# Other columns for the operands of the last nine passes of a decoder step, one pass with a gap in its columns and one with its products in another order

## The chip, the cores and the metric

The kernel runs on one core of a Trainium2 chip. The metric is the time of one execution on the device in microseconds, measured over several runs of the whole program; three runs of the kernel before gave 1616.21, 1616.83 and 1617.44 us, with a median of 1616.83 us.

## The reference

One layer of a decoder for a group of 256 prompt tokens and a group of 32 sample tokens, 288 rows in all, with a model width of 2048. What bears on the change is its end:

```python
merged = gates[:, :, 0] * y_conv + gates[:, :, 1] * y_sb + gates[:, :, 2] * y_mem
x = x + merged @ p['w_o']
h2 = rms_norm(x, p['g_mlp'])
x = x + jnp.square(jax.nn.relu(h2 @ p['w_up'])) @ p['w_down']
```

`w_o` is 2048 by 2048, `w_up` 2048 by 8192 and `w_down` 8192 by 2048. Before these lines stand the combined projection, a convolution branch, stick-breaking attention and attention into a memory, none of which the change touches.

## The kernel before

All activations are held transposed: 128 features on the partitions, the 288 tokens along the columns (T = 288). A product of 128 output features is one "tile": 16 blocks of 128 input features, each with a 128x128 block of weights as the stationary operand and the 128x288 activations as the moving operand, accumulated in one bank of PSUM.

The weights are kept in float32 in HBM and TensorE is used in its fp32r type, so every operand is split in a high part (rounded to fp32r) and a low part (the rest). Each block of a tile is three matmuls: high weights by high activations, high weights by low activations, low weights by high activations. A slab is 8 blocks of weights side by side (128 x 1024 columns, 512 KB); there are 504 of them, and each is loaded by a DMA from SP's queue into a buffer `wr` (line 285), rounded on ScalarE into `wh` (line 307), and subtracted on VectorE into `wl` (line 318). `wr`, `wh` and `wl` have four buffers each. The generator `products` (line 544) issues a slab's 24 matmuls through `chunk` (line 536, the matmul is line 538): first the 16 with `wh`, going through the blocks with the high and the low activations in turn, then the 8 with `wl`. A tile of the last passes is two slabs, 48 matmuls.

The last nine passes are the output projection (`out_tile`, line 1388, 16 tiles) and, for each of four quarters c = 0 to 3 of the 8192 hidden features, an up pass (`up_tile`, line 1423, 16 tiles) and a down pass (`down_tile`, line 1441, 16 tiles). An up tile is evacuated by VectorE (line 1427, relu and scale), squared on GpSimd (line 1430), rounded to the high part on ScalarE (line 1433), and its low part is taken on VectorE (line 1435). These two parts are the moving operands of the down pass that follows. They lie in 16 pairs of "homes" that `make_homes` (line 1327) cuts out of two older buffer pools, `k4` (ten tiles of 1024 columns, three homes in each, 320 columns apart) and `s` (eight tiles of 512 columns, one home in each). The output projection's moving operands lie in the same homes, written by `branch` (line 1354). The moving operands of the up passes are the normalised activations `h2`, in tiles `a` of 320 columns.

Where in these buffers an operand starts is set by constants (line 176 and line 179): `AHEAD = 4` is the first column in a tile `a`, `HOME = 36` the first column of a home, and `SHIFT = 5` the first column of a slab's parts in `wh` and `wl` (line 288, tiles of 1088 columns), except for the 16 slabs of the memory stage, which start at column 0. In the memory stage (line 591) the roles are turned: the weights are the moving operand, 512 columns wide, and the activations, from column 32 of their tiles, are stationary.

The order of all instructions is worked out before the program is built: generators ask a planner (`Order`) for time on an engine, with costs such as `MM = 0.131` us per matmul, and the planner puts each engine's instructions in a fixed order. A matmul group is planned no earlier than the flags of the operands it uses: both parts of its slab and its activations.

Of the kernel before, what the change touches and what calls it, by code (L numbers as in the profile page):

```python
# [8 lines left out]
F32R = mybir.dt.float32r  # L9
# [6 lines left out]
P = 128  # L16
D_MODEL = 2048
KT = D_MODEL // P
# [4 lines left out]
T = NP + NS  # L23
# [14 lines left out]
N_SLABS = 504  # L38
# [134 lines left out]


APART = 320
AHEAD, HOME = 4, 36
PAD = 64
GRP = 32
SHIFT = 5
MM = 0.131  # L180
MM_MEM = 0.226

# [2 lines left out]
def tile_decoder_step(ctx: ExitStack, tc: tile.TileContext, xT, memT, wall, cvec, kmat, ptab,  # L185
                      kpool, vpool, mkc, mvc, hist,
                      yT, oK, oV, oCp, oCs, oMK, oMV):
    nc = tc.nc
# [20 lines left out]
    def tl(p, shape, dt=F32):  # L209
        cnt[0] += 1  # L210
        return pools[p].tile(shape, dt, tag=p, name=f"{p}_{cnt[0]}")
# [27 lines left out]
    first = cm[:, C_BGATE:C_BGATE + 2 * ML].rearrange("p (k t) -> p k t", k=2)  # L239
# [31 lines left out]
    class Slab:  # L271
        def __init__(self, parts):
            self.parts = parts
            self.landed = [Flag() for _ in range(parts)]
            self.split = [Flag() for _ in range(parts)]
# [11 lines left out]

    def shifted(p, s):
        n = 0 if s < 2 * KT // 2 else SHIFT
        return tl(p, [P, SLAB + PAD], F32R)[:, n:n + SLAB]  # L290

    def due(s):
# [242 lines left out]

    def chunk(ps, todo, first, last):
        for i, (w, a) in enumerate(todo):
            nc.tensor.matmul(ps, w, a, start=(first and i == 0), stop=(last and i == len(todo) - 1))  # L538

    slab_no = [0]  # L540
    FULL = [k * P for k in range(8)]
# [2 lines left out]
    def products(ps, uses, acts, first=True, last=True, n=T):  # L544

        s = slab_no[0] - 1
        sl = slabs[s]
        high = [(sl.h, c, a, x) for c, a in zip(uses, acts) for x in (0, 1)]
        low = [(sl.l, c, a, 0) for c, a in zip(uses, acts)]
        todo = high + low  # L550
        for i in range(0, len(todo), STEP):
            part = todo[i:i + STEP]
            yield pe(len(part) * MM, *sl.split, *{a.flag for _, _, a, _ in part})
            if i == 0 and first:
                start_slab(s)
            chunk(ps, [(w[:, c:c + P], a.l if x else a.h) for w, c, a, x in part],
                  first and i == 0, last and i + STEP >= len(todo))

    def main_tile(acts, evac, rank=1.0, n_slabs=2):
        yield pe(0.0, pm=1)  # L560
        ps = bank("pm")[:, :T]
        for i in range(n_slabs):
            slab_no[0] += 1
            yield from products(ps, FULL, acts[8 * i:8 * i + 8], i == 0, i == n_slabs - 1)
            give("w")
        add(evac(ps), rank)
# [754 lines left out]
    homes, homes_in = [], Flag()  # L1321

    class Home:
        def __init__(self, h, l):
            self.h, self.l = h, l

    def make_homes():
        yield sp(*conv_done, *osb_in, k4=bufs["k4"], s=bufs["s"])
        parts = []
        for _ in range(bufs["k4"]):  # L1330
            x = tl("k4", [P, 1024], F32R)
            parts += [x[:, HOME + i * APART:HOME + i * APART + T] for i in range(3)]
        for _ in range(bufs["s"]):
            parts.append(tl("s", [P, 512], F32R)[:, HOME:HOME + T])
        for j in range(KT):
            homes.append(Home(parts[2 * j], parts[2 * j + 1]))
        done(homes_in)


# [12 lines left out]
    merged = [None] * KT  # L1352

    def branch(br, j):
        def evac(ps):
            sig = gates[br, j]
            if br == 2:
                yield dve(T, sig.flag, a=1)
                macc[j] = tl("a", [P, T])
                nc.vector.tensor_mul(macc[j], ps, sig.out)  # L1360
                give("pm")
                give("t")
                return
            yield dve(T, sig.flag)
            nc.vector.tensor_mul(sig.out, ps, sig.out)
            give("pm")
            yield dve(T)
            nc.vector.tensor_add(macc[j], macc[j], sig.out)
            give("t")
            if br == 0:  # L1370
                yield act(T, homes_in)
                a = merged[j] = homes[j]
                nc.scalar.copy(a.h, macc[j])
                yield dve(T)
                nc.vector.tensor_sub(a.l, macc[j], a.h.bitcast(F32))
                give("a")
                done(merged_in[j])
        return evac
# [41 lines left out]
        return load, evac  # L1420


    def up_tile(u, f):
        def evac(ps):
            yield dve(T, r2_done, t=1)
            r = tl("t", [P, T])
            nc.vector.scalar_tensor_tensor(r, ps, 0.0, r2, op0=ALU.max, op1=ALU.mult)  # L1427
            give("pm")
            yield pool(T)
            nc.gpsimd.tensor_mul(r, r, r)  # L1430
            yield act(T)
            a = homes[f]
            nc.scalar.copy(a.h, r)  # L1433
            yield dve(T)
            nc.vector.tensor_sub(a.l, r, a.h.bitcast(F32))  # L1435
            give("t")
            u[f].h, u[f].l = a.h, a.l
            done(u[f].flag)
        return evac
# [57 lines left out]
    def main():  # L1497
        yield from warm_up()
        yield from mem_products()
        yield from conv_products([evac_lin(0, "pa"), evac_gat(0, "pa"), evac_lin(1, "pm"), evac_gat(1, "pm")])  # L1500
        for j in range(2, CT):
            yield from main_tile(hx, evac_lin(j, "pm"))
            yield from main_tile(hx, evac_gat(j, "pm"))
        add(samples(), 2.3)
        for h in range(MH):
            yield from main_tile(hx, mem_head(h), 2 + 0.05 * h)
        for h in range(SH):
            yield from main_tile(hx, sb_key(h), 2.2 + 0.05 * h)
            yield from main_tile(hx, sb_query(h), 2.2 + 0.05 * h)
            yield from main_tile(hx, sb_head(h), 2.2 + 0.05 * h)  # L1510
        yield from branch_products(2, [Late(omem, h, om_in[h]) for h in range(MH)])
        give("a", 8)
        yield from branch_products(1, [Late(osb, h, osb_in[h]) for h in range(SH)])
        give("a", 16)
        yield from branch_products(0, [Late(cact, j, cact_flags[j]) for j in range(CT)])
        give("a", 40)
        mg = [Late(merged, j, merged_in[j]) for j in range(KT)]
        for j in range(KT):
            load, evac = out_tile(j)
            add(load(), 2)  # L1520
            yield from main_tile(mg, evac)
        add(after(sums_2, x1_norm), 0.4)
        hh = [Late(h2, j, h2_in[j]) for j in range(KT)]
        for c in range(D_FF // D_MODEL):
            u = [Later() for _ in range(KT)]
            for f in range(KT):
                yield from main_tile(hh, up_tile(u, f))
            for j in range(KT):
                yield from main_tile(u, down_tile(j, c == D_FF // D_MODEL - 1))

# [167 lines left out]
```

## Time and profile before

| what | value |
|---|---|
| median of three runs | 1616.83 us |
| the profiled execution | 1617.72 us |
| its span, first to last instruction | 1615.9 us |
| PE busy | 1610.4 us, 12638 matmuls |
| VectorE busy | 978.3 us |
| ScalarE busy | 752.6 us |
| GpSimd busy | 139.6 us |
| mean of the DMA traffic | 192 GB/s |

The profile is of one execution. Its span leaves out some 1.8 us of the execution's own time, before the first and after the last instruction. Rows of the views name an engine, a line of the kernel, the operation and its operands as output <- inputs by the names of their pools. For `pm<-k,wh` the output is a bank of the pool `pm`, the moving operand lies in a tile of `k4` and the stationary operand in `wh`. "PEld" is the loading of a stationary operand, which is recorded beside the matmul. The recorded length of a matmul is from its start to its last result, and matmuls overlap; how many follow each other in how much time is read from their starts. A timeline row gives the start, the length, the engine and how many alike instructions were merged in it.

### The profile page before, as it was taken

To read this page: it belongs to the slowest core of one execution; us is meant where nothing else is said; L and a number is where in the kernel's file an instruction comes from. 1 tells how busy PE (TensorE), PEld (TensorE's weight loads), DVE (VectorE), ACT (ScalarE), POOL (GpSimd) and SP (SyncE) were. 2 spreads that over 40 slices of the span, in tenths; PEclk is the share of its full clock that TensorE was granted. 3 is DMA by queue.
4 is the path that set the end of the run, shared out by engine and by line. 5 is a ranking of instruction groups with operands and counts; after the bars stand their busy time and mean duration, and the time that the engine had idled before them with its cause. 6 is when DMAs were issued, how large, how long until landed. Compare 5 with 4: busy or idle time off the path is not lost.

```text
span 1615.9 us, 30749 instructions
## 1 busy us (share of the span) xinstructions
PE 1610.4 (100%) x12638; PEld 1592.4 (99%) x12638; DVE 978.3 (61%) x1503; ACT 752.6 (47%) x1078; POOL 139.6 (9%) x106
## 2 busy tenths in 40 slices
PE   9999999999999999999999999999999999999999
PEld 7999999999999999999999999999999999999999
DVE  7889888877777655655555544555445554455443
ACT  8856877654334534444443333333333333333332
POOL 0020000000000000002222100121002210022100
PEclk9999999999999999999999999999999999999999
DMA  9887778987755555466655555555555555555562
GB/s 326 231 198 267 201 256 237 323 225 271 220 170 166 173 169 170 151 195 191 193 171 167 170 170 169 168 170 171 169 170 170 170 170 169 171 167 169 180 194 95
DMA packets 127200, 310.25 MB, mean 192 GB/s; under 512 B 40018, under 2 KB 49618, under 8 KB 127058
## 3 DMA queue, kind: packets, MB, share of 16 engines
q1 hardware_dynamic: 126770, 307.98, 61.2%
q8 instruction: 99, 1.62, 0.4%
q10 hardware_dynamic: 288, 0.29, 0.1%
q14 instruction: 43, 0.35, 0.1%
HBM read 296.99 MB, written 6.32 MB: 188 GB/s over the span
## 4 chain that ended last, share of the span: by engine, by line
PE 97%; DVE 1%; DMA 1%; issue 0%; ACT 0%; SPq 0%; DVEq 0%; ACTq 0%
PE pm L538 91%; PE pm L591 3%; DMA wr<-in_wall 1%; PE pa L538 1%; PE pl L1090 1%; DVE wl L318 1%; PE pl L1274 0%; PE pa L917 0%; PE pa L919 0%; PE pa L918 0%; PE pl L1104 0%; DVE a L770 0%; PE pa L1214 0%; PE pa L1250 0%; ACT wh L307 0%
## 5 line engine op out<-in xcount | busy, mean ns | idle before, releaser
L307 ACT CAST wh<-wr 128x1024 fp32r<-128x1024 f32 (+1 forms) x520 | 529.2, 1022 | 643.3 <-PE pm L538 570.6
L318 DVE TENSOR_TENSOR wl<-wr,wh 128x1024 fp32r<-128x1024 f32 (+1 forms) x520 | 618.2, 1193 | 192.6 <-ACT wh L307 189.6
L538 PE MATMUL pm<-a,wh 128*128 128x288 f32 x5184 | 733.9, 292 | 0.0
L538 PEld LDWEIGHTS pm<-a,wh 128*128 128x128 f32 x5184 | 695.2, 188 | 1.4 <-issue 1.0
L538 PE MATMUL pm<-a,wl 128*128 128x288 f32 x2592 | 394.9, 292 | 0.0
L538 PEld LDWEIGHTS pm<-a,wl 128*128 128x128 f32 x2592 | 358.0, 188 | 0.0
L538 PE MATMUL pm<-k,wh 128*128 128x288 f32 x2400 | 338.0, 292 | 0.0
L538 PEld LDWEIGHTS pm<-k,wh 128*128 128x128 f32 x2400 | 321.6, 188 | 0.0
L538 PE MATMUL pm<-k,wl 128*128 128x288 f32 x1200 | 181.8, 292 | 0.0
L538 PEld LDWEIGHTS pm<-k,wl 128*128 128x128 f32 x1200 | 165.4, 188 | 0.0
L1430 POOL TENSOR_TENSOR t<-t 128x288 f32<-128x288 f32 x64 | 96.7, 1510 | 599.2 <-DVE t L1427 599.2
L1444 DVE TENSOR_TENSOR a<-a,pm 128x288 f32<-128x288 f32 x64 | 29.0, 454 | 122.7 <-PE pm L538 122.7
L1427 DVE SCALAR_TENSOR_TENSOR t<-pm,rx 128x288 f32<-128x288 f32 x64 | 29.3, 457 | 92.1 <-PE pm L538 92.1
L1433 ACT CAST k<-t 128x288 fp32r<-128x288 f32 x60 | 26.0, 433 | 126.0 <-POOL t L1430 126.0
L1346 DVE TENSOR_TENSOR t<-pm,rx 128x288 f32<-128x288 f32 x48 | 22.0, 458 | 71.8 <-PE pm L538 71.8
L1435 DVE TENSOR_TENSOR k<-t,k 128x288 fp32r<-128x288 f32 x60 | 28.0, 466 | 59.4 <-ACT k L1433 59.4
L770 DVE SCALAR_TENSOR_TENSOR a<-a,cv,a 128x256 f32<-128x256 f32 x120 | 59.5, 496 | 1.4
L1416 POOL TENSOR_TENSOR t<-t,t 128x288 f32<-128x288 f32 x15 | 21.9, 1462 | 413.9 <-ACT t L1413 413.9
L591 PE MATMUL pm<-wh,a 128*128 128x512 f32 x128 | 34.8, 392 | 0.5 <-ACT wh L307 0.5
L538 PE MATMUL pm<-s,wh 128*128 128x288 f32 x160 | 33.8, 292 | 0.0
L591 PEld LDWEIGHTS pm<-wh,a 128*128 128x128 f32 x128 | 24.1, 190 | 6.5 <-ACT wh L307 1.6
L538 PEld LDWEIGHTS pm<-s,wh 128*128 128x128 f32 x160 | 25.6, 188 | 0.0
(181 smaller groups left out, 707.7 us busy)
## 6 DMA issues: line engine op xcount, KB each, us to landing
wr<-in_wall SPq DMA_DIRECT2D x488, 512.0 KB, 3.7
wr<-in_wall SPq DMA_DIRECT2D x32, 256.0 KB, 5.1
k<-in_kpool SPq DMA_DIRECT2D x32, 256.0 KB, 5.9
k<-in_vpool SPq DMA_DIRECT2D x32, 256.0 KB, 5.9
k<-in_mkc SPq DMA_DIRECT2D x8, 512.0 KB, 8.9
k<-in_mvc SPq DMA_DIRECT2D x8, 512.0 KB, 8.2
t<-in_xT SPq DMA_DIRECT2D x16, 144.0 KB, 3.7
out_yT<-a SPq DMA_DIRECT2D x16, 144.0 KB, 1.9
```

The lines of the kernel that those rows point to most:

```text
L307: nc.scalar.copy(sl.h[:, c], sl.raw[:, c])
L318: nc.vector.tensor_sub(sl.l[:, c], sl.raw[:, c], sl.h[:, c].bitcast(F32))
L538: nc.tensor.matmul(ps, w, a, start=(first and i == 0), stop=(last and i == len(todo) - 1))
L591: nc.tensor.matmul(ps[m], y[:, m * P:(m + 1) * P], z[:, w], start=(k == 0 and j < 2), stop=(k == KT - 1 and j in (4, 5)))
L770: nc.vector.scalar_tensor_tensor(c[:, :NP], up[:, k:k + NP], w, c[:, :NP], op0=ALU.mult, op1=ALU.add)
L1346: nc.vector.tensor_mul(g, ps, rx)
L1416: nc.gpsimd.tensor_add(sq_sum[0], sq_sum[0], res[0])
L1427: nc.vector.scalar_tensor_tensor(r, ps, 0.0, r2, op0=ALU.max, op1=ALU.mult)
L1430: nc.gpsimd.tensor_mul(r, r, r)
L1433: nc.scalar.copy(a.h, r)
L1435: nc.vector.tensor_sub(a.l, r, a.h.bitcast(F32))
L1444: nc.vector.tensor_add(x1[j], x1[j], ps)
```

## The change

Six things are changed, all in the last nine passes.

- A home is now 320 columns, starting at column 32 of its slot, and each pass says where in it the operand starts. The output projection's operands start 12 columns in. The four down passes start at 0, 4, 8 and 16 columns in.
- The weights of these passes are shifted along: 13 columns for the output projection, and one more than the activations for the down passes, so 1, 5, 9 and 17.
- The weights of the first up pass start at column 37 in place of 5; the other three up passes keep 5.
- In the second down pass (c = 1) the 288 moving columns have a gap: 144 columns, 16 unused ones, 144 columns. ScalarE and VectorE write them so, and the matmul reads them and writes PSUM with a two-part pattern (PSUM itself has no gap).
- In the last quarter (c = 3, up and down) the 24 products of a slab come in another order: for each block high weights by high activations, low weights by high activations, high weights by low activations, where before all 16 with the high weights came ahead of the 8 with the low ones.
- `HOME` goes from 36 to 32, which is part of the first point.

```diff
-AHEAD, HOME = 4, 36
+AHEAD, HOME = 4, 32
...
+FF0 = N_SLABS - 4 * 4 * KT
+OUT_AT = 12
+DOWN_AT = (0, 4, 8, 16)
+DOWN_GAP = (0, 16, 0, 0)
+UP_SHIFT = (37, 5, 5, 5)
...
     def shifted(p, s):
         n = 0 if s < 2 * KT // 2 else SHIFT
+        if FF0 - 2 * KT <= s < FF0:
+            n = OUT_AT + 1
+        elif s >= FF0:
+            c, i = divmod(s - FF0, 4 * KT)
+            n = UP_SHIFT[c] if i < 2 * KT else DOWN_AT[c] + 1
         return tl(p, [P, SLAB + PAD], F32R)[:, n:n + SLAB]
...
-            nc.tensor.matmul(ps, w, a, start=(first and i == 0), stop=(last and i == len(todo) - 1))
+            nc.tensor.matmul(like(ps, a), w, a, start=(first and i == 0), stop=(last and i == len(todo) - 1))
...
         todo = high + low
+        if s >= FF0 + 3 * 4 * KT:
+            todo = [x for i, y in enumerate(low) for x in (high[2 * i], y, high[2 * i + 1])]
...
     class Home:
-        def __init__(self, h, l):
-            self.h, self.l = h, l
+        def __init__(self, j, at, gap=0):
+            self.h, self.l = (apart(x[:, at:at + T], gap) for x in homes[j])
+
+    def apart(x, gap):
+        if not gap:
+            return x
+        return bass.AP(tensor=x.tensor, offset=x.offset, ap=[list(x.ap[0]), [T // 2 + gap, 2], [1, T // 2]])
+
+    def like(x, a):
+        return x if len(a.shape) == 2 else x.rearrange("p (i t) -> p i t", i=2)
...
-                a = merged[j] = homes[j]
+                a = merged[j] = Home(j, OUT_AT)
...
-            a = homes[f]
+            a = Home(f, DOWN_AT[c], DOWN_GAP[c])
+            r = like(r, a.h)
```

More of the change, by code (lines that the diff above doesn't have):

```diff
@@ L1331, in make_homes @@
             x = tl("k4", [P, 1024], F32R)
-            parts += [x[:, HOME + i * APART:HOME + i * APART + T] for i in range(3)]
+            parts += [x[:, HOME + i * APART:HOME + (i + 1) * APART] for i in range(3)]
         for _ in range(bufs["s"]):
-            parts.append(tl("s", [P, 512], F32R)[:, HOME:HOME + T])
+            parts.append(tl("s", [P, 512], F32R)[:, HOME:HOME + APART])
         for j in range(KT):
-            homes.append(Home(parts[2 * j], parts[2 * j + 1]))
+            homes.append(parts[2 * j:2 * j + 2])
         done(homes_in)
@@ L1420, in out_tile, with up_tile @@
         return load, evac
-    def up_tile(u, f):
+    def up_tile(u, f, c):
         def evac(ps):
@@ L1526, in main @@
             for f in range(KT):
-                yield from main_tile(hh, up_tile(u, f))
+                yield from main_tile(hh, up_tile(u, f, c))
             for j in range(KT):
```

## Prediction, made before the changed kernel was run

> **What bounds the kernel now.** I read the page first (who is busy, which chain ended last), then the chain of waits in order of time and PE's waits, then the busy time by passes.
>
> ```profile
> span 1615.9 us, 30749 instructions
> PE 1610.4 (100%) x12638; PEld 1592.4 (99%) x12638; DVE 978.3 (61%) x1503; ACT 752.6 (47%) x1078; POOL 139.6 (9%) x106
> PE 97%; DVE 1%; DMA 1%; issue 0%; ACT 0%; SPq 0%; DVEq 0%; ACTq 0%
> L538 PEld LDWEIGHTS pm<-a,wh 128*128 128x128 f32 x5184 | 695.2, 188 | 1.4 <-issue 1.0
> ```
>
> PE is busy for the whole span and carries 97% of the chain. A busy PE says little by itself, since overlapping matmuls count as busy; whether it waits is seen in the next two views, the chain and PE's waits.
>
> ```profile
> 422.81 3.70 PE pl L1090 x128
> 426.52 1185.81 PE pm L538 x9120
> 1612.35 0.46 DVE a L1444
> PE pa L1494 <- PEq L1675: 0.8, 1, 0.8
> PE pa L919 <- DVE a L898: 0.7, 1, 0.7
> PE pm L591 <- ACT wh L307: 0.5, 2, 0.3
> ```
>
> From 426.52 us to the end the chain is one piece: 9120 matmuls of line 538 in 1185.81 us, which is 130.02 ns each, and then one evacuation. PE waits three times in the whole program, all earlier. So the only thing that can move this kernel's end, as long as no new wait appears, is how fast one matmul follows another. The windows view, cut at the nine changed passes (output projection, then up and down four times), shows that rate for each pass:
>
> ```profile
> 713.59:813.43 99.84, 99.84 (x770) 99.84 (x769) 1.00 0.61 193
> 813.43:913.27 99.84, 99.84 (x770) 99.84 (x769) 1.00 0.54 168
> 913.27:1013.12 99.85, 99.85 (x771) 99.85 (x770) 1.00 0.54 170
> 1013.12:1112.95 99.83, 99.83 (x770) 99.83 (x769) 1.00 0.54 168
> ...
> 1512.31:1612.15 99.84, 99.84 (x770) 99.78 (x768) 1.00 0.50 159
> ```
>
> The columns are the stretch, its length, PE's and PEld's busy time, the granted clock, the DMA share and GB/s. Each pass takes 99.84 us for its 16 x 48 = 768 matmuls (the x770 counts the ones that overlap an edge): 130.0 ns each, at the full clock, whatever else is going on. The nine passes are 6912 matmuls and 898.6 us, so **one ns per matmul in all of them is 6.9 us (0.43%), in one pass 0.77 us**. About 0.2%, 3.2 us, is what a measurement of this kernel can tell from no change.
>
> **Part by part: places of the columns.** Nothing is added or removed: the same 6912 matmuls read the same number of columns. What can change is the 130.0 ns, if it depends on where the moving columns and the columns being loaded as stationary operand lie. By the code all tiles concerned are multiples of 64 columns wide (1024, 512, 320 apart, 1088, 320), so every buffer of a pool has the same place modulo 64. The kernel before holds three arrangements, as stationary start less moving start: 5 - 4 = 1 in the up passes, 5 - 36 = -31 in the output projection and the down passes, and 32 - 0 in the memory stage. The windows show the first two equal to 0.01 us in a pass, and that over every k, s and a buffer. For the third there is the timeline of the memory stage:
>
> ```profile
> 19.98 1.07 PE L591 MATMUL pm<-wh,a 128*128 128x512 f32 x4
> ...
> 44.45 1.07 PE L591 MATMUL pm<-wh,a 128*128 128x512 f32 x4
> ```
>
> Between these two rows lie 18 groups of 6 matmuls (4 with the weights' high part, 2 with the low): 24.47 us / 108 = 226.6 ns for 512 columns, 0.4425 ns a column, against 130.0 / 288 = 0.4514. A straight line through both is 5.8 ns fixed and 0.4313 ns a column. So no arrangement in this trace is visibly dearer.
>
> After the change the difference is 13 - 44 = -31 for the output projection, 1 - 32, 5 - 36, 9 - 40 and 17 - 48 = -31 for the down passes, all as before: both operands are moved together, by +8, -4, 0, +4 and +12 columns. The first up pass goes from 1 to 37 - 4 = 33, which modulo 64 is the -31 that the down passes run at already. If it is the difference that counts, these edits cost nothing. That the common place doesn't count is not shown by any row, since the trace has only starts 4, 36 and 0 for the moving columns. Bounds: if the new places freed all of the fixed part that the memory row suggests, a matmul would take 288 x 0.4425 = 127.4 ns, 2.6 ns less, 2.0 us a pass. If they brought a collision that kept a load from lying beside the matmul ahead of it, the 188 ns of the LDWEIGHTS row would be the least, 58 ns more, 44.5 us a pass; that is far from anything seen, since 188 is a recorded length with its start and end, and PEld is 99% busy at 130 ns all the same. I take 0, since the three arrangements seen are nearest.
>
> **The gap.** In the second down pass the moving operand is 2 x 144 columns. The nearest rows are two products with samples, both 64 matmuls with 32 stationary and 256 moving columns; line 1104 reads the 256 in one piece, line 1274 in two pieces of 128 that lie apart:
>
> ```profile
> 148.36 3.66 PE L1104 MATMUL pl<-k,k 128*32 128x256 f32 x64
> 296.92 3.64 PE L1274 MATMUL pl<-k,k 128*32 128x256 f32 x64
> ```
>
> 3.64 us against 3.66: two pieces cost nothing, down to 0.3 ns a matmul. Paid once more at the worst, the fixed 5.8 ns would be 4.5 us for the pass. I take 0.
>
> **The order in the last quarter.** Its loads alternate between wh and wl where before the same wh block was loaded twice in a row. Within a slab before, both kinds already stand: 16 matmuls in which the stationary block repeats and 8 in which it never does.
>
> ```profile
> 1509.19 2.24 PE L538 MATMUL pm<-a,wh 128*128 128x288 f32 x16
> 1511.27 1.20 PE L538 MATMUL pm<-a,wl 128*128 128x288 f32 x8
> 1512.31 2.24 PE L538 MATMUL pm<-k,wh 128*128 128x288 f32 x16
> ```
>
> From start to start 2.08 us / 16 and 1.04 us / 8: 130.0 ns both. So the order costs nothing in rate; bounds as above, by 2.6 ns x 1536 = 4.0 us either way. It also shifts two waits. wl of a slab is needed by its 2nd matmul, not its 17th, 15 x 0.13 = 2.0 us earlier. And the last use of wh is the 24th matmul, not the 16th, so that ScalarE's rounding of the slab four later, which waits for that buffer, starts up to 8 x 0.13 = 1.04 us later. Queued behind it in order are the rounding of an up tile (line 1433) and the next slab's; VectorE's subtraction, and with it the wr buffer for SP's next DMA, follow it. The timeline about the last pass's start gives the cover:
>
> ```profile
> 1461.55 1.05 ACT L307 CAST wh<-wr 128x1024 fp32r<-128x1024 f32 x1 [1.67 <-PE pm L538]
> 1462.97 1.22 DVE L318 TENSOR_TENSOR wl<-wr,wh 128x1024 fp32r<-128x1024 f32 x1
> 1471.75 2.24 PE L538 MATMUL pm<-a,wh 128*128 128x288 f32 x16
> 1514.66 0.43 ACT L1433 CAST s<-t 128x288 fp32r<-128x288 f32 x1 [2.14 <-POOL t L1430]
> 1515.13 0.46 DVE L1435 TENSOR_TENSOR s<-t,s 128x288 fp32r<-128x288 f32 x1 [1.02 <-ACT s L1433]
> 1517.25 0.42 PE L538 MATMUL pm<-s,wh 128*128 128x288 f32 x2
> ```
>
> The slab rounded at 1461.55 has its low part at 1464.19 and is used from 1471.75: 7.6 us, of which at most 1.04 go with the later start, and the 2.0 us of wl's earlier need have no bearing, as the slab's first matmul already stands 7 us behind. The ACT rows show 1.67 and 2.14 us idle ahead of these instructions, which take up the shift, so the up tile's rounding stays where GpSimd lets it go. The last up tile's parts are ready at 1515.59 and read from 1517.25; in the new order their block is the 45th and not the 39th in the pass's first tile, 0.8 us later, so the slack grows. For the loads:
>
> ```profile
> wr<-in_wall SPq DMA_DIRECT2D x488, 512.0 KB, 3.7
> ```
>
> A wr buffer set free at 1464.19 + 1.04 is filled again 3.7 us after its issue, about 1469, for a rounding at 1461.55 + 4 x 3.12 = 1474.0. Were all this cover gone, it would cost up to 1.04 us at each of the 64 slabs; with 5 us left I take 0.
>
> **The sum** is 0 + 0 + 0 against the profiled execution's 1617.72 us (span 1615.9 and 1.8 around it), which is 0.9 above the median of the runs. Carried to the median: **1616.8 us**.
>
> **The rivals.** (a) *The common place counts, for the worse.* In the passes where both operands are moved or split (output projection and four down passes, 3840 matmuls) the moving stream and the load behind it meet. Price: the only difference per matmul that placements show here, 2.6 ns, the other way, is 10.0 us, 1626.8; with the gap at 5.8 in place of 2.6 ns it is 12.4 us, 1629.2. It decides from 3.2 us / 3840 = 0.84 ns a matmul. For it: starts 0, 8, 12 and 16 stand in no row. Against it: starts 4 and 36, and k, s and a buffers, agree to 0.01 us in a pass. (b) *The common place or the order frees some of the fixed part.* The same 3840 matmuls at -2.6 ns give -10.0 us, 1606.8; the last quarter's order alone -4.0 us, 1612.8. For it: 512 columns take less per column. Against it: that is explained as well by a fixed part that no place removes. The Trainium skill ("TensorE: Matmul & The Clock Gate", Back-to-back issue gap) puts a warm gap at N / 2.4 + 2.5 ns, an estimate of 122.5 ns for 288 columns; by that, 7.5 of the 130.0 ns could go, 29 us in these passes, 1588. The trace disagrees with it in every arrangement (226.6 ns for 512 columns against 215.8), so I give such a gain hardly anything. (c) *The change doesn't do what it says*, as the difference modulo 64 stays -31 nearly everywhere: this has the same time as my forecast and is counted in it.
>
> **How the numbers follow.** No change 0.50, since every row at hand gives 130.0; (a) 0.27, as the new common places are untested and the starting one is at least not bad; (b) 0.23. That gives faster 0.23, same 0.50, slower 0.27. The forecast's own range is 1613.6 to 1620.0. The whole range goes from (b)'s 1606.8 to (a)'s 1629.2: it leaves out a collision much dearer than 2.6 ns (about 0.10) and a gain as large as the far part of (b) (about 0.08).
>
> **What would show it.** Right: windows cut at the passes again give 99.84 us each, in all nine, and PE waits nowhere after 426 us. Wrong by (a) or (b): single passes differ, those moved in common from the two up passes that are left alone (c = 1 and 2), and the windows name the pass: 97.8 us for -2.6 ns, 101.8 for +2.6. If the first up pass alone differs, modulo 64 was the mistake; if the last up pass differs, which has only the new order, the order was; if only the gap's pass does, the two-piece read. A wait of PE on wl or wh in the last quarter would prove the cover wrong.

## The result, and the profile after

The changed kernel takes 1630.68 us in the median of four runs (1630.51 to 1631.61), the kernel before, with a fourth run added, 1616.66 us: a ratio of 1.0087, with a 95% interval of 1.0075 to 1.0099. It is 14.0 us slower. The forecast was no change, and the time lies 1.5 us above the range.

The page's head, then the end of the chain and all of PE's waits:

```profile
span 1629.8 us, 30749 instructions
PE 1624.0 (100%) x12638; PEld 1606.4 (99%) x12638; DVE 982.3 (60%) x1503; ACT 754.2 (46%) x1078; POOL 126.0 (8%) x106
```

```profile
426.65 1199.65 PE pm L548 x9120
```

```profile
PE pa L931 <- DVE a L910: 1.5, 1, 1.5
PE pa L1515 <- PEq L1696: 0.8, 1, 0.8
```

The number of instructions is the same, the last piece of the chain is again 9120 matmuls in one run, and PE waits for nothing after 426 us: of its two waits one is the first matmul's, at 0.8 us, and the other ends at 128.35 us. But the piece is 13.84 us longer, 131.5 ns a matmul in place of 130.0. Where, the windows show, cut at the starts of the nine passes (output projection, then up and down for c = 0 to 3; stretch, length, PE and PEld busy, clock, DMA share, GB/s):

```profile
713.73:813.58 99.85, 99.85 (x771) 99.85 (x769) 1.00 0.61 193
813.58:915.98 102.40, 102.40 (x771) 102.40 (x770) 1.00 0.53 165
915.98:1018.38 102.40, 102.40 (x771) 102.40 (x770) 1.00 0.53 165
1018.38:1118.21 99.83, 99.83 (x770) 99.83 (x769) 1.00 0.55 169
1118.21:1221.64 103.43, 103.43 (x771) 103.43 (x770) 1.00 0.53 164
1221.64:1321.48 99.84, 99.84 (x770) 99.84 (x769) 1.00 0.54 168
1321.48:1423.88 102.40, 102.40 (x770) 102.40 (x769) 1.00 0.52 166
1423.88:1523.73 99.85, 99.85 (x771) 99.85 (x769) 1.00 0.55 168
1523.73:1626.12 102.39, 102.39 (x770) 102.32 (x768) 1.00 0.49 156
```

Four passes are as before, 130.0 ns a matmul: the output projection at columns 12 and 13, the two up passes that were left alone, and the last up pass, which has only the new order. Four others take 102.40 us, 133.33 ns: the first up pass with its weights at 37, and the down passes at 0, 8 and 16. The pass with the gap takes 103.43 us, 134.67 ns. 4 x 2.56 + 3.59 = 13.8 us, the whole of the 13.84 us. The clock is at its full rate in every row.

**A count that has to be put right first.** The prediction counted columns inside the tiles. In the addresses that the built program carries, the tiles of `k4` and `s` begin at byte 136128 and 177088, those of `wh` and `wl` at 193472 and 210880, all 48 columns past a multiple of 64 (256 bytes), but those of `a` at 27456, 16 past one. So a home at column 36 and an `a` operand at column 4 are the same place modulo 64: both moving starts are 20, and the stationary start is 53. Before the change all nine passes had one arrangement, a distance of 33 from moving to stationary start. After it the distance is 33 again except in the first up pass, where it is 1, and the moving starts are 28 (output projection), 16, 20, 24 and 32 (down passes). Below, a pair such as (20, 53) is moving and stationary start by this count.

### The profile page after: what moved, and what is told of

It is laid out like the page before. It is cut to its first block, busy times and chain, and to the rows that moved or that the text cites. A ratio compares the mean times of both kernels' runs of the same rounds, so it can differ in the third digit from the quotient of the medians.

```text
span 1629.8 us, 30749 instructions
## 1 busy us (share of the span) xinstructions
PE 1624.0 (100%) x12638; PEld 1606.4 (99%) x12638; DVE 982.3 (60%) x1503; ACT 754.2 (46%) x1078; POOL 126.0 (8%) x106
## 4 chain that ended last, share of the span: by engine, by line
PE 97%; DVE 1%; DMA 1%; ACT 1%; issue 0%; SPq 0%; DVEq 0%; ACTq 0%
PE pm L548 91%; PE pm L603 3%; PE pa L548 1%; PE pl L1102 1%; DVE wl L328 1%; DMA wr<-in_wall 1%; PE pl L1286 0%; PE pa L1515 0%; PE pa L929 0%; PE pa L931 0%; ACT wh L317 0%; PE pa L930 0%; PE pl L1116 0%; DMA a<-in_hist 0%; DVE a L782 0%
## 5 line engine op out<-in xcount | busy, mean ns | idle before, releaser
L548 PE MATMUL pm<-a,wh 128*128 128x288 f32 x5184 | 763.9, 293 | 0.0
L548 PEld LDWEIGHTS pm<-a,wh 128*128 128x128 f32 x5184 | 709.6, 188 | 1.4 <-issue 1.0
L548 PE MATMUL pm<-a,wl 128*128 128x288 f32 x2592 | 432.1, 293 | 0.0
L548 PE MATMUL pm<-k,wh 128*128 128x288 f32 x2400 | 374.5, 296 | 0.0
L548 PEld LDWEIGHTS pm<-a,wl 128*128 128x128 f32 x2592 | 371.4, 188 | 0.0
L548 PEld LDWEIGHTS pm<-k,wh 128*128 128x128 f32 x2400 | 340.2, 188 | 0.0
L548 PE MATMUL pm<-k,wl 128*128 128x288 f32 x1200 | 219.5, 296 | 0.0
L548 PEld LDWEIGHTS pm<-k,wl 128*128 128x128 f32 x1200 | 179.8, 188 | 0.0
L1450 POOL TENSOR_TENSOR t<-t 128x288 f32<-128x288 f32 x64 | 83.1, 1298 | 623.2 <-DVE t L1447 623.2
```

Of the source, the lines that this page charges most:

```text
L548: nc.tensor.matmul(like(ps, a), w, a, start=(first and i == 0), stop=(last and i == len(todo) - 1))
```

## The experiments

For these the stationary start got a constant of its own beside the moving start; every diff stands against the changed kernel with that done. The diffs are cut to the constants that matter and written in shorthand, with `none` for no gap. The order of the products is the old one in all passes, except in e4 and e11 (new in the last quarter, as in the changed kernel) and e14 (new in all quarters). One kernel has nine passes, so it measures up to nine arrangements. Times of a pass come from its windows in one profiled execution, a rate is that time over 768. Times of the whole kernel are given for e4, e11, e12 and e15, which had 8 to 10 runs each; the others had one. In e6, e7 and e9 the kernel computes something else, so that only the rates of their passes mean anything.

**e1, one operand moved at a time.**

```diff
-OUT_AT, OUT_SHIFT = 12, 13
-DOWN_AT, DOWN_SHIFT = (0, 4, 8, 16), (1, 5, 9, 17)
-DOWN_GAP, UP_SHIFT = (0, 16, 0, 0), (37, 5, 5, 5)
+OUT_AT, OUT_SHIFT = 12, 5
+DOWN_AT, DOWN_SHIFT = (0, 8, 16, 20), (5, 5, 5, 5)
+DOWN_GAP, UP_SHIFT = none, (1, 4, 6, 7)
```

> One operand is moved at a time, so that the start of the moving columns and that of the stationary ones come apart. Pairs are (column in the home, column in the slab): output projection (12, 5), down passes (0, 5), (8, 5), (16, 5), (20, 5); the up passes keep their moving columns and take the weights from column 1, 4, 6 and 7 in place of 5. Theory M, the place of the moving columns within 8 (32 bytes) decides, 4 is good and 0 is bad: 102.40 us for the down passes (0, 5), (8, 5) and (16, 5), 99.84 for (12, 5), (20, 5) and all four up passes. Theory S, the place of the stationary columns within 8 decides, 5 is good and 1 is bad: 99.84 us for the output projection and all four down passes, 102.40 for the first up pass. Theory D, only the distance of the two starts decides, whatever their common place: then each of these passes may have a time of its own, and the two passes whose distance is the same, (8, 5) and the up pass with 1, agree.

```profile
712.46:814.85 102.39, 102.39 (x771) 102.39 (x769) 1.00 0.61 188
814.85:915.72 100.87, 100.87 (x771) 100.87 (x769) 1.00 0.54 167
...
1120.53:1222.93 102.40, 102.40 (x770) 102.40 (x769) 1.00 0.53 166
...
1427.72:1527.57 99.85, 99.85 (x771) 99.85 (x770) 1.00 0.54 169
```

The output projection (28, 53) is dear although (28, 61) cost nothing, so the moving place alone (theory M) is out. The down passes with weights at 5, (16, 53), (24, 53), (32, 53) and (36, 53), all take 102.4 us, so the stationary place alone (theory S) is out. One column more or less at the weights is enough: the up passes at 4 and 6 take 102.40 us, at 7 99.85. And (20, 49) and (24, 53), with the same distance of 29, take 100.87 and 102.40, so the distance alone (theory D) is out as well.

**e2, the weights through the multiples of 8.**

```diff
+OUT_AT, OUT_SHIFT = 4, 37
+DOWN_AT, DOWN_SHIFT = (4, 4, 4, 4), (61, 1, 9, 13)
+DOWN_GAP, UP_SHIFT = none, (21, 29, 45, 53)
```

> Moving columns stay where they were in all nine passes, and the weights go through the multiples of 8 away from column 5, and two places between: up passes 21, 29, 45 and 53, output projection 37, down passes 61, 1, 9 and 13. Theory S (place within 8): 99.84 us for 13, 21, 29, 37, 45, 53 and 61, 102.40 for 1 and 9. Theory M (only the moving columns' place counts): 99.84 us everywhere, which the first up pass of the changed kernel, 102.40 us with its weights at 37, speaks against. Theory D (the distance counts, modulo 64 columns or less): 102.40 us for 37 again, now in the output projection, and for those of the others whose distance falls in the same part; 99.84 us for a connected range around 5. A control for the tiles: 37 in the homes gives the same as 37 in the other activations.

```profile
713.23:815.63 102.40, 102.40 (x771) 102.40 (x770) 1.00 0.61 188
...
1020.41:1120.28 99.87, 99.87 (x770) 99.87 (x769) 1.00 0.54 169
1120.28:1221.15 100.87, 100.87 (x770) 100.87 (x769) 1.00 0.55 168
1221.15:1320.99 99.84, 99.84 (x770) 99.84 (x769) 1.00 0.54 168
```

The weights at 37 are dear with the homes too, so it is the place and not the tile: (20, 21) is 102.40 us whether the moving columns lie in `a` or in `k4` and `s`. Likewise (20, 49) is 100.87 us in e1's up pass and here in a down pass. Of the starts a multiple of 8 away from 5, 29 and 45 are as good as 5; 21, 37, 53 and 61 take 102.4 us and 13 takes 101.1. Theory S, which had all of 13 to 61 at 99.84 us, is out once more. There is no connected good range.

**e3, gaps.**

```diff
+OUT_AT, OUT_SHIFT, OUT_GAP = 4, 5, 24
+DOWN_AT, DOWN_SHIFT = (4, 4, 4, 4), (5, 5, 5, 5)
+DOWN_GAP, UP_SHIFT = (0, 4, 8, 32), (2, 3, 8, 0)
```

> Both operands where they were before the change; the moving columns are cut in two pieces of 144 with a gap of 24 columns in the output projection and of 0, 4, 8 and 32 in the down passes; a gap of 0 is the two-piece pattern without any gap. Theory P, the two-piece pattern costs by itself: 103.42 us (134.67 ns a matmul) in all five. Theory G, the second piece has its own place against the stationary columns and costs by that: 99.84 us for the gap of 0, and more for the others by their size, with 4 and 8 unlike each other. The up passes scan the weights' start at 2, 3, 8 and 0 in place of 5: theory D (distance) says 99.84 us for 2 and 3 and possibly more at 0 and 8; theory S says 102.40 for 0 and 8 at the least.

```profile
916.17:1016.02 99.85, 99.85 (x770) 99.85 (x769) 1.00 0.55 169
...
1119.69:1222.09 102.40, 102.40 (x770) 102.40 (x769) 1.00 0.54 165
...
1325.53:1428.78 103.25, 103.25 (x771) 103.25 (x770) 1.00 0.52 164
...
1528.62:1630.01 101.39, 101.39 (x770) 101.31 (x768) 1.00 0.49 157
```

The four rows are gaps of 0, 4, 8 and 32. Two pieces without a gap cost nothing; a gap costs 1.5 to 3.4 us, and 24 in the output projection 2.5. Theory P is out. The second piece has another place against the weights, as theory G says. The up passes, with weights from 2, 3, 8 and 0, took 101.55, 103.67, 103.44 and 99.84 us: neither theory's figures for them hold, since S had the start at 0 dear and D had 2 and 3 at 99.84 us.

**e4, the harmless two.**

```diff
-DOWN_AT, DOWN_SHIFT = (0, 4, 8, 16), (1, 5, 9, 17)
-DOWN_GAP, UP_SHIFT = (0, 16, 0, 0), (37, 5, 5, 5)
+DOWN_AT, DOWN_SHIFT = (4, 4, 4, 4), (5, 5, 5, 5)
+DOWN_GAP, UP_SHIFT = none, (5, 5, 5, 5)
```

> Only the two edits stay of which the profile of the changed kernel showed passes of 99.84 us: the output projection at columns 12 and 13, and the new order of the products in the whole last quarter. The first up pass and the four down passes are as before, without a gap. If the loss is a sum over passes, the time is that of the kernel before, ratio 1.000 within 0.001, and the last down pass with the new order takes 99.84 us. If the order costs in a down pass, it takes 102.40 us and the kernel 2.5 us more; if the edits act together, part of the 14 us is still there.

```profile
1511.13:1610.98 99.85, 99.85 (x770) 99.77 (x768) 1.00 0.51 160
```

The row is the last down pass, with the new order. 1616.61 us, ratio 1.0002 (0.9992 to 1.0011); all nine passes take 99.84 or 99.85 us. So the loss is a sum over passes, and neither the output projection's move by 8 nor the order costs anything at these places.

**e5, both moved by 8.**

```diff
+OUT_AT, OUT_SHIFT = 20, 21
+DOWN_AT, DOWN_SHIFT = (12, 12, 12, 12), (8, 15, 11, 16)
+DOWN_GAP, UP_SHIFT = none, (10, 12, 15, 17)
```

> Places are now counted as the allocator gave them, modulo 64 columns (256 bytes): the homes' tiles begin at 48, the tiles of the up passes' activations at 16, the slabs at 48. By this count the kernel before had one arrangement in all nine passes: moving 20, stationary 53, distance 33. Theory D8: the time depends on the distance modulo 64 and on the moving start modulo 8, so that a common move by 8 changes nothing and one by 4 does. It says: output projection moving 36, stationary 5 (distance 33) 99.84 us; down passes at moving 28 with distances 28, 35, 31 and 36 the same as measured at moving 20: 99.85, 99.84, 103.67 and 103.43 us. Theory A, every pair of absolute places has its own time: these five would be scattered between 99.84 and 103.7 without agreement. The up passes (weights from 10, 12, 15 and 17; distances 38, 40, 43 and 45) go on with the scan: if 130.0 ns is a floor, none is under 99.84 us.

```profile
712.10:811.95 99.85, 99.85 (x770) 99.85 (x769) 1.00 0.62 192
...
914.36:1014.21 99.85, 99.85 (x770) 99.85 (x769) 1.00 0.55 169
...
1316.30:1419.98 103.68, 103.68 (x770) 103.68 (x769) 1.00 0.53 163
...
1521.10:1624.54 103.44, 103.44 (x770) 103.34 (x768) 1.00 0.50 154
```

All five came out as theory D8 had them from other starts: 99.85, 99.85, 99.85, 103.68 and 103.44 us. A common move by 8 columns changed nothing in these five pairs, with good and with bad distances. The up passes, weights from 10, 12, 15 and 17, took 102.41, 99.84, 102.40 and 101.12 us.

**e6, one stream of reads standing still.** By pass, the moving operand, the stationary one or both are read with stride 0.

```diff
+            how = MODES[...]   # None, moving x2, stationary x2, both x2, None x2
+            chunk(ps, [trim(w[:, c:c + P], a.l if x else a.h, how) for w, c, a, x in part], ...)
+    def still(x, n):
+        return bass.AP(tensor=x.tensor, offset=x.offset, ap=[list(x.ap[0]), [0, n]])
```

> Part of the computation is changed: in the first quarter's two passes every matmul reads the first moving column 288 times (stride 0), in the second quarter's the first stationary column is loaded 128 times, in the third quarter's both. Weights start at 5 in the up passes (the good arrangement) and at 37 in the first two down passes (133.33 ns when nothing stands still). Theory C, the two streams of reads get in each other's way by their places: with one stream standing still the passes with 5 and with 37 come out alike, and with both still the rate is at its best, 288 columns at the slope of 0.4313 ns, 124.2 ns or 95.4 us, or still lower. Theory F, the 10 ns over the columns are a fixed cost of a matmul and places only add to it: 99.84 us with a still operand, with 5 and with 37. Rival N, the places of the operands have nothing to do with one another: the still passes keep 99.84 and 102.40. The last up pass (weights from 49, distance 13) and the last down pass (moving 24, stationary 56, distance 32) are two more points of the scan.

```profile
712.34:812.18 99.84, 99.84 (x770) 99.84 (x769) 1.00 0.62 192
812.18:906.26 94.08, 94.08 (x770) 94.08 (x769) 1.00 0.58 179
906.26:1000.34 94.08, 94.08 (x770) 94.08 (x769) 1.00 0.59 180
1000.34:1099.67 99.33, 99.33 (x770) 99.33 (x769) 1.00 0.56 170
1099.67:1199.00 99.33, 99.33 (x771) 99.33 (x769) 1.00 0.57 171
1199.00:1293.08 94.08, 94.08 (x771) 94.08 (x770) 1.00 0.59 179
```

With the moving operand still, a matmul takes 122.5 ns, with the weights at 5 and at 37 alike, and the same with both still. With the stationary operand still it takes 129.33 ns, again the same for both places, which differ by 3.3 ns when nothing stands still. So the difference between these two places needs both streams; and of the 130.0 ns at the best places 7.5 are not a fixed part of a matmul but come with the moving columns being really read. Theory F is out, N too; C is right: the places come out alike, and with both still the rate is 122.5 ns, below its 124.2, as its "or still lower" left open. The two further pairs took 101.12 us (20, 33) and 102.40 us (24, 56).

**e7, fewer columns.**

```diff
+MODES = (256, 256, 224, 224, 192, 192, 160, 160, None)
+        return w, a[:, :how] if how else a
```

> Part of the computation is left out: all matmuls of a tile but its first work on the first 256, 224, 192 or 160 columns in place of 288. Each width stands once in the good arrangement (distance 33) and once in the bad one (distance 1): output projection 256 bad, then 256 good, 224 good, 224 bad, 192 bad, 192 good, 160 good, 160 bad; the last down pass has 288 columns at distance 1, in the homes. Theory F (a fixed part of 5.8 ns and 0.4313 ns a column): 116.2, 102.4, 88.6 and 74.8 ns good, unless the loading of 128 stationary columns sets a bound, and 3.3 ns more in the bad one at each width. Theory C (collisions along the stream): the difference between bad and good shrinks with the width or changes its sign from width to width. A bound by the load would show as one rate for all widths under some width. The last down pass takes 102.40 us, as the up pass and the output projection with 37 did.

```profile
712.14:802.01 89.87, 89.87 (x770) 89.87 (x769) 1.00 0.70 213
802.01:892.78 90.77, 90.77 (x771) 90.77 (x770) 1.00 0.60 186
892.78:978.85 86.07, 86.07 (x770) 86.07 (x769) 1.00 0.65 196
```

At 256 columns the arrangement that is bad at 288 is the better one, 89.87 against 90.77 us: the sign turns with the width, as collisions along the stream would have it and a price per matmul would not. At 224, 192 and 160 columns every pass takes 86.07 or 86.08 us, 112.1 ns on average (the first matmul of each tile, one in 48, still reads all 288 columns), in both arrangements: there something that doesn't depend on the width is the bound. The load of the 128 stationary columns would do that; no run here shows that it is the load. The last down pass, (20, 21) at full width, took 102.42 us, as expected.

**e8, moving starts at 16.**

```diff
+OUT_AT, OUT_SHIFT = 0, 60
+DOWN_AT, DOWN_SHIFT = (0, 0, 0, 0), (0, 3, 2, 4)
+DOWN_GAP, UP_SHIFT = none, (11, 14, 20, 33)
```

> The moving columns start at 16 modulo 64 (a multiple of 8) in the output projection and the down passes, with stationary starts that give distances of 28, 32, 35, 34 and 36. The five pairs with a moving start at a multiple of 8 so far (distances 21, 29, 33 three times, 37) all took 133.3 ns. Theory M8: a moving start at a multiple of 8 costs 133.3 ns whatever the distance, 102.40 us for all five. Theory D8 without that: distances 28 and 35, which give 99.84 us at moving 20, may do so here as well, and 34 and 36 differ. The up passes (weights from 11, 14, 20 and 33; distances 39, 42, 48 and 61 at moving 20) go on with the scan: if 130.0 ns is a floor, none is under 99.84 us.

```profile
914.10:1016.50 102.40, 102.40 (x770) 102.40 (x769) 1.00 0.55 165
...
1321.85:1422.55 100.70, 100.70 (x771) 100.70 (x770) 1.00 0.55 168
...
1523.82:1623.66 99.84, 99.84 (x770) 99.77 (x768) 1.00 0.52 159
```

Distances 32, 34 and 36 here; 28 and 35 took 101.55 and 101.84. A moving start at a multiple of 8 is not dear by itself (theory M8 is out): (16, 52) is here as good as any. The up passes, weights from 11, 14, 20 and 33, took 99.85, 101.13, 102.38 and 101.27 us.

**e9, other orders of reading.**

```diff
+MODES = ((4, 1), (1, -1), (1, -1), (2, 1), (1, -1, "out"), (8, 1), (1, -1), (1, -1), (1, -1))
+        return bass.AP(tensor=x.tensor, offset=x.offset + at, ap=[list(x.ap[0]), [step, n]])
```

> Can the collisions of the two streams be thinned out? Part of the computation is changed in every pass: the moving columns are read from the last to the first (first up pass with weights from 5, first down pass from 37, third down pass from 13, fourth up pass from 21, fourth down pass from 0; in the second down pass from 5, and there PSUM is written backwards as well, which undoes it), or the 128 stationary columns are read with a step of 4 (output projection), 2 (second up pass) or 8 columns (third up pass), as if the blocks of a slab were laid out in turn. Theory C, the 7.5 ns over the 122.5 that a still moving operand gives are collisions whose number hangs on the relative motion of the streams: the reversed passes are unlike 130.0 and 133.3 ns, some under 130.0, and with a step of 8 the loaded columns sweep eight times as far, so the time changes as well. Theory F2, 130.0 ns is the floor as soon as the moving stream really reads 288 different columns: no pass under 99.84 us (129.33 ns, 99.33 us, with a still stationary operand is the one exception so far).

```profile
712.17:892.86 180.69, 180.69 (x771) 180.69 (x769) 1.00 0.36 109
...
1096.37:1198.88 102.51, 102.51 (x771) 102.51 (x769) 1.00 0.54 164
...
1301.27:1486.66 185.39, 185.39 (x770) 185.39 (x769) 1.00 0.30 93
```

Stationary columns read with a step of 4, 2 and 8: 235, 133.5 and 241 ns a matmul. Moving columns read backwards take 100.70 to 102.39 us. Nothing came under 99.84 us, as theory F2 had it. Of theory C's forecasts the larger step did change the time, but no backward pass came under 130.0 ns, and two of them stood at 133.3 ns, where it had them all unlike that.

**e10, moved together by less than 4.**

```diff
+OUT_AT, OUT_SHIFT = 3, 4
+DOWN_AT, DOWN_SHIFT = (5, 6, 7, 2), (6, 7, 8, 3)
+DOWN_GAP, UP_SHIFT = none, (18, 22, 24, 26)
```

> Both operands are moved together, at the old distance of 33, by -1 (output projection), 1, 2, 3 and -2 columns (down passes). Known are 0 and 8 and 16: 99.84 us, and -4, 4 and 12: 102.40 us. Theory D8 (distance, and moving start modulo 8) leaves these open; if what counts is which line of 16 or 32 bytes the start lies in, a move by 1, 2 or 3 (moving starts 5, 6 and 7 modulo 8) is near 99.84 us and -1 and -2 (starts 3 and 2) near 102.40; if the exact column counts, they scatter. The up passes scan on at moving 20 (weights from 18, 22, 24 and 26, distances 46, 50, 52 and 54): with a floor of 130.0 ns none is under 99.84 us.

```profile
712.05:811.89 99.84, 99.84 (x770) 99.84 (x769) 1.00 0.62 192
...
914.30:1019.25 104.95, 104.95 (x770) 104.95 (x769) 1.00 0.54 161
```

Moved by -1: 99.84 us, by +1: 104.95, the dearest of all with both operands whole and read forwards in one step. By 2 it is 103.71, by 3 100.93, by -2 102.40. They scatter; lines of 16 or 32 bytes don't order them. The up passes, weights from 18, 22, 24 and 26, took 102.41, 101.76, 99.84 and 101.56 us.

**e11, the new starts with other partners.**

```diff
-DOWN_SHIFT, DOWN_GAP, UP_SHIFT = (1, 5, 9, 17), (0, 16, 0, 0), (37, 5, 5, 5)
+DOWN_SHIFT, DOWN_GAP, UP_SHIFT = (4, 5, 12, 20), two pieces without a gap in c = 1, (45, 5, 5, 5)
```

> The changed kernel with all its new moving starts (12 in the output projection, 0, 4, 8, 16 in the down passes), the two-piece pattern in the second down pass (with a gap of 0) and the new order in the last quarter, but with the stationary starts of the dear passes chosen for the pair: 45 for the first up pass (distance 9), 4, 12 and 20 for the down passes at 0, 8 and 16 (distance 36 and a moving start at a multiple of 8, of which only the first was measured). Theory D8 (distance modulo 64 and moving start modulo 8): all nine passes take 99.84 us and the time is that of the kernel before, ratio 1.000 within 0.001. If absolute places count, the down passes at 8 and 16 are dearer, up to 2.6 us each and 5 us in all.

```profile
811.97:914.80 102.83, 102.83 (x771) 102.83 (x770) 1.00 0.52 164
...
1314.16:1414.00 99.84, 99.84 (x770) 99.84 (x769) 1.00 0.55 170
...
1513.86:1614.57 100.71, 100.71 (x770) 100.63 (x768) 1.00 0.50 158
```

1620.62 us, ratio 1.0026 (1.0015 to 1.0037): 10 of the 14 us are gone. The down passes at 0 and 8 are at 99.84 us with their new partners. But (20, 29) takes 102.83 where e2 had 99.84, and (32, 4) 100.71. D8 as a rule with one time for each case falls. The 131.1 ns of (32, 4) may be its place or, at this point, the new order.

**e12, the gap alone.**

```diff
+DOWN_AT, DOWN_SHIFT, DOWN_GAP = (4, 4, 4, 4), (5, 5, 5, 5), (none, 16, none, none)
+OUT_AT, OUT_SHIFT, UP_SHIFT = 4, 5, (5, 5, 5, 5)
```

> Only the gap of 16 columns in the second down pass, everything else as before. If the loss of the changed kernel is a sum over its passes, this pass takes 103.42 us, the others 99.84 us, and the whole kernel 3.6 us more than before, ratio 1.0022. If the passes act on one another, or the profile of one execution doesn't carry over to the runs, the ratio lies apart from that by more than its interval.

```profile
1111.59:1214.99 103.40, 103.40 (x770) 103.40 (x769) 1.00 0.55 164
```

1619.83 us, ratio 1.002 (1.001 to 1.003), the other passes at 99.84 or 99.85: a pass's profile carries over to the runs.

**e13, one pair four times.**

```diff
+UP_SHIFT, DOWN_AT, DOWN_SHIFT = (45, 45, 45, 45), (4, 4, 4, 4), (5, 1, 13, 5)
```

> All four up passes with their weights from 45 (moving 20, stationary 29, distance 9), after passes of different rhythm: the output projection at 4 and 5, then down passes at (4, 5), (4, 1) and (4, 13), known at 130.0, 131.3 and 131.7 ns. Theory H, a pair of places can settle in more than one rhythm and what runs ahead of it chooses: the first two up passes, which follow 130.0 ns, take 102.8 us as in the repaired kernel, the third, after (4, 1), 99.84 us as in the scan. Theory D8 (one time for each distance and start modulo 8): all four the same, and then the 102.83 us of the repaired kernel came from something else.

```profile
812.55:912.39 99.84, 99.84 (x770) 99.84 (x769) 1.00 0.56 169
...
1012.23:1112.07 99.84, 99.84 (x770) 99.84 (x769) 1.00 0.55 168
...
1212.94:1315.76 102.82, 102.82 (x770) 102.82 (x769) 1.00 0.53 163
...
1416.88:1519.71 102.83, 102.83 (x771) 102.83 (x769) 1.00 0.54 164
```

The same pair (20, 29) runs at 130.0 ns twice and at 133.9 twice in one execution. So a pair can have two rhythms. Theory H is right in that, but wrong in which: here the passes at 133.9 ns come after those of 131.3 and 131.7 ns, in e11 it came after a pass at 130.0, and in e2 the pass at 130.0 came after 131.3. What chooses is not the rate of the pass ahead: (20, 49) at 131.3 ns stood ahead of a pass at 130.0 ns in e2 and of one at 133.9 ns here. The starts of the single matmuls show the two rhythms. In the two passes at 130.0 ns the steps from start to start alternate between 128 and 132 ns from the first matmul on; in the two at 133.9 ns they go through a cycle of twelve steps, from 128 to 142 ns, over and over, as in e11.

**e14, the new order in all quarters.**

```diff
+MIXED = (0, 1, 2, 3)
+DOWN_AT, DOWN_SHIFT, UP_SHIFT = (0, 8, 16, 0), (4, 12, 20, 1), (5, 0, 7, 5)
```

> The new order of the products in all four quarters; up passes with weights from 5, 0, 7 and 5, down passes at (0, 4), (8, 12), (16, 20) and (0, 1). In the old order these pairs were measured at 130.0 ns, the last at 133.3 in both orders' neighbourhood, and (16, 20) only in the new order, 131.1. Theory O, the order is harmless everywhere: 99.84 us in every pass but (0, 1), which has 102.40, and (16, 20), which may show 100.6 again. Theory H, the order shifts which rhythm a pair settles in: some of the passes with 0, 7, (0, 4) or (8, 12) leave 99.84 us.

```profile
912.08:1012.78 100.70, 100.70 (x770) 100.70 (x769) 1.00 0.55 168
...
1312.32:1412.17 99.85, 99.85 (x771) 99.85 (x769) 1.00 0.55 169
```

Now (16, 52) takes 100.70 us and (32, 4) 99.85, the other way round than in e11; (16, 49) is 102.40 in both orders; the other six passes are at 99.84 or 99.85.

**e15, the repaired kernel with two edits taken back.**

```diff
+MIXED, UP_SHIFT = (), (5, 5, 5, 5)   # against e11
```

> The repaired kernel once more, with the two edits whose passes were not at 99.84 us taken back: the first up pass with its weights from 5, and the old order in the last quarter. All new moving starts (12; 0, 4, 8, 16) and the two-piece pattern without a gap stay, with stationary starts 13, 4, 5, 12 and 20. If starts at a multiple of 8 are harmless with the right partner: all nine passes 99.84 us, ratio 1.000 within 0.001. If (16, 20) is dear by its place and not by the order, its pass takes 100.6 us again, 0.7 us in all.

```profile
1511.33:1612.03 100.70, 100.70 (x770) 100.63 (x768) 1.00 0.49 158
```

1617.76 us, ratio 1.0006 (0.9996 to 1.0015), which includes no change. (32, 4) takes 100.70 us again, now in the old order; in the new one it has had 100.71 and 99.85. So for (32, 4) the order doesn't choose between the two rhythms. For (16, 52), the same distance of 36, that isn't settled: its three passes in the old order took 99.84 or 99.85 us, its only one in the new order 100.70. The other eight passes are at 99.84 to 99.86. No kernel here beats the one before.

## Why the prediction was wrong

**What bounds the kernel** was right: of the 13.9 us by which the span grew, 13.84 are the matmuls' rate, and no wait appeared in these passes. (The row of line 591 counts two waits, so PE waited four times before the change, not three; all lie ahead of 426 us.)

**The step that failed is the one on the places of the columns**: "The kernel before holds three arrangements", two of them equal to 0.01 us in a pass, and so "I take 0, since the three arrangements seen are nearest". Tiles of one pool do have the same place modulo 64, but the pools' bases are 32 columns apart, so the two arrangements that agreed were one and the same, (20, 53). The agreement that carried the forecast was empty. By address the memory stage was the one other arrangement, and it has 512 moving columns, so that it compares widths. In place of 0, four moved passes measured 3.33 ns a matmul (2.56 us each). The same slip made the first up pass look like a known case; it had the distance 1, not seen before, and took 133.33 ns. And "both operands are moved together", which I held for harmless if the difference counts, was harmless by 8 (e4, e5) but not by -4, +4 or +12.

**The gap**: that two pieces cost nothing was right (99.85 us without a gap), that the gap then costs nothing was wrong: the pass took 4.67 ns a matmul more, alone as well (e12), and by an amount that hangs on the gap's size (e3), which fits the other place that it gives half of the columns.

**The order** was right in rate and cover: 99.85 us in the last up pass, 99.85 in the last down pass of e4, and the shifted waits stayed hidden. (The block of the last up tile is the 46th in the new order, not the 45th; the slack grew as forecast.)

**Rival (a)**, that the places count for the worse through the moving stream and the load behind it, was nearest, with its price mis-sized: 2.6 ns against a measured 3.33, and 5.8 for the gap against 4.67. It had the output projection in it, which costs nothing, and lacked the first up pass, and its sum came to 12.4 us in place of 14.0. That the two lie so close is luck: the pass that it had too many stands in for the one that it lacked, and its high price for the gap makes up for part of its low price for the places. Its 2.6 ns were the wrong yardstick: they compare widths, not places.

**The rule from the Trainium skill** left room for a gain, to which I gave hardly anything, and none came. Still, the estimate of 122.5 ns for 288 columns by the Trainium skill's formula ("TensorE: Matmul & The Clock Gate", Back-to-back issue gap), which the page gives for an isolated matmul, is what e6 shows, 94.08 us / 768 = 122.5, as soon as the moving operand stands still. What the same page of the Trainium skill says in its step-by-step part, that loading the next weights "doesn't steal SBUF read bandwidth from the running matmul", fits these runs badly: the rate hangs on the pair of places, and at the two places tested it no longer does when either stream stands still (e6). That it is bandwidth which the load takes is not shown.

**Shown, and what stays open.** Shown: the loss is the sum of five slower passes; it hangs on the places of both operands together; the difference between (20, 53) and (20, 21) vanishes where one stream stands still; a common move by 8 columns kept the rate in the five pairs of e5, though not always among (16, 52), (24, 60) and (32, 4), of which two have two rates. That the streams meet in some part of the memory is the reading that fits, but which part and by what rule isn't shown. No rule in distances or lines that I tried gives the times. Three pairs ran at two rates, from the first slab of a pass to its last, and what chooses between them is open.

## What to carry to other kernels

Where matmuls follow each other without a gap, the columns at which the two operands start can matter: up to 5% here, with fp32r operands and 288 moving columns (130.0 to 136.7 ns), and no difference between the two places tried at 224 columns and fewer. That is worth a scan in one kernel with a different pair in each pass, since each pass shows its own rate in the windows. Here the kernel before already stood at the best rate found. Count places by the address, not inside the tile, and a view in which two cases agree is evidence only after it is clear that they are two. Prefer a pair that gave the same rate wherever it stood: (20, 53), whole and read forwards at 288 columns, did so in every pass that had it.

## What the runs showed of the hardware that was not expected

- Reading both operands in full, no pass of 288 columns came under 130.0 ns a matmul; some 7.5 ns over the 122.5 of a still moving operand are left at the best places found.
- Rates are locked: many different pairs give 130.0 or 133.3 ns for a whole pass, and one column at one operand goes from the one to the other, (20, 53) to (20, 52). The starts repeat in a short cycle: two steps at 130.0 ns, and at 133.3 ns two for (20, 21) but five for (16, 49), alike to within 2 ns.
- A stationary operand read with a step of 4 or 8 columns (16 or 32 bytes) makes a matmul of 288 columns take 235 or 241 ns; a step of 2 takes 133.5 ns. That agrees with the Trainium skill ("SBUF — State Buffer", Specifications), which asks for at least two hits in each 16-byte line.
- At 224, 192 and 160 columns a matmul with its load took 112.1 ns on average (one in 48 at full width), at both places tried.
